# The last column block of a fused block's closing FFN: its products kept in row-block order, with the gate's row and two gated tiles prepared at other places

## The chip, the cores and the metric

The kernel runs on one core of one Trainium2 chip. The metric is the device time of one execution in microseconds (us). The median of three runs of the kernel before is 1876.98 us (1876.95 to 1877.79).

## The reference

A residual block works on x of 256 tokens by 2048 channels, in float32: a SwiGLU feed-forward, a mixer (mLSTM heads beside RG-LRU channels), and a second SwiGLU feed-forward. Each sublayer is modulated by shift, scale and gate computed from a conditioning vector c, and followed by a layer norm. What matters here is the second feed-forward and the norm that ends the block:

```python
g, v = jnp.split(u @ w13, 2, axis=-1)          # u = modulate(x, 2), w13: 2048 x 11264
y = (jax.nn.silu(g) * v) @ w2                  # w2: 5632 x 2048
x = _layer_norm(ALPHA * x + 0.5 * gate[:, 2] * y, ln_g[l, 2], ln_b[l, 2])
```

## The kernel before

Each float32 operand of a large product is split into a high part (a cast to fp32r on ScalarE, ACT) and a low part (the difference, on VectorE, DVE). A product of two operands is then three matmuls on TensorE (PE): high x high, high x low, low x high. A weight tile is 128 x 2048. It is loaded by a transfer that SyncE (SP) issues into a `raw` buffer (four of them) and split into a `hi` and a `lo` buffer (three of each).

`last_ffn` is the second feed-forward. Its 5632 hidden columns are 11 groups of 512. The tokens are two row blocks t = 0, 1 of 128 rows. `u2` holds the normalized, modulated and transposed input, as `uh` (high) and `ul` (low), 16 tiles of 128 channels. Groups 2 to 10 are computed by a Strassen-like scheme (`fast_group`). A string of steps gives PE's order within a group: `P1` to `P7` are sub-products of twelve matmuls each, `G` and `V` are plain sub-products of the gate's and value's columns (24 matmuls each), `X` takes a down tile of w2 (24 matmuls) from earlier groups, and `t` transposes a finished part of the hidden activations. `P1` reads u's tiles 0 to 3, `P2` and `P4` tiles 4 to 7, `G` 8 to 11, `V` 12 to 15; the other P's read sums of u that were made once before. Within a group, P1's raw tile sits in a `row` buffer (two of these; the modulation row and the gate's row take one each while they live) and is overwritten to make P5's, P6's and P4's operands, so it is free once P4's operand is split.

The order of the other engines' work in `last_ffn` comes from a planner, `Plan`, that runs when the kernel is built. Each operation is given with an engine (`T` PE, `V` DVE, `A` ACT, `G` POOL, `Q` SP), an assumed duration, what it reads and writes, and sometimes a due time (`by`). PE's operations keep the order in which they are written. For the others the planner works back due times from PE's, then schedules by list: among operations that could start, the one due first. It knows how many buffers of each kind there are. A load is assumed to land after 5.6 us (`LAND`). Each engine then gets its instructions in the order of the planned starts, and executes them in that order; nothing on the chip reorders between them. Instructions issued through `T`, `V`, `A`, `G` or `Q` are pinned to the written order. Those issued through `nc.tensor` are not: a scheduler orders them at build time by a simulated time line.

The output has four column blocks n of 512. Down tiles (n, k) of the last three groups (k = 0, 1, 2 for groups 8, 9, 10) are accumulated for n = 0, 1, 2 inside `last_ffn` (`end_tile`), multiplied by the gate, added to `yacc` (the residual, itself scaled by the gate and with alpha times x accumulated from DRAM), and their statistics are taken. For n = 3 the three weight tiles are multiplied by the gate's row (`gated`, and the lines after it for k = 0, as `l0`), split, and kept: k = 0 in `hi`/`lo` buffers, k = 1 and k = 2 in the place of `u2`, one half by row block each. The products of n = 3 are made in `boundary` (`last`, calling `mov_t`): `products(0)` for row block 0, then `products(1)`, 36 matmuls each. After a row block's products, DVE adds the sum to `yacc` (here also named x), takes statistics, and normalizes (`take`, `norm`), and the result goes out by eight transfers in all. For row block 1, two of its four columns are normalized through PE: `tz` receives x times ln_g through the identity, and then minus the mean times ln_g through a diagonal matrix `dm`, which ACT builds once the mean is known.

The gate's row (`gate_row`) is a PE transpose of the gate's columns, a scaling on ACT, and two transfers issued by POOL, through DRAM, that broadcast it to all partitions.

Of the kernel before, what the change touches and what calls it, by code (L numbers as in the profile page):

```python
# [44 lines left out]
DOUBLE = ()  # L45
ADA_END = 6
SLOT_END = 45.0
ADA_AT = tuple(2.0 + 8.0 * i for i in range(7)) + tuple(130.0 + 20 * i for i in range(9))

S4 = "P1 t X t P5 X P6 P3 X P7 P2 G P4 G X V V"  # L50
S2 = "P1 t G t P5 X P6 P3 G P7 P2 X P4 V V"
D6 = "P1 t X t P5 X P6 P3 X P7 P1 P2 X P5 P4 X P6 P3 P2 X P7 P4"


# [11 lines left out]

class Place:

    def __init__(self, tag, make, ap=None):
        self.tag, self.make, self.ap = tag, make, ap  # L70
        self.left, self.end, self.also, self.whole = 0, None, [], None

    def __call__(self):
        if self.ap is None:
            self.ap = self.make()
        return self.ap


# [9 lines left out]
class Plan:  # L88
# [11 lines left out]
        self.now = 0.0  # L100

    def place(self, tag, make, ap=None):
        p = Place(tag, make, ap)
        if ap is not None and tag:
            self.taken[tag] += 1
        return p

    def part(self, whole, key, make):
# [7 lines left out]
    def op(self, engine, dur, fn, reads=(), writes=(), moves=0.0, seq=None, by=None, at=None):  # L116
        s = Step(engine, dur, fn, moves)
        s.by = None if by is None else self.now + by
        s.at = at
        if engine == "T":  # L120
            s.due = self.now
            self.now += dur
            seq = "T"
        if seq:
            if seq in self.seq:
                s.order.add(self.seq[seq])
            self.seq[seq] = s
        keys = [[k for x in ks for k in (x, *(x.also if isinstance(x, Place) else ()))] for ks in (reads, writes)]
        for k in keys[0]:
            if k in self.last:  # L130
                s.before.add(self.last[k])
        for k in keys[1]:
            s.before.update(self.seen.get(k, ()))
            if k in self.last:
                s.before.add(self.last[k])
        for k in keys[0]:
            self.seen.setdefault(k, []).append(s)
        for k in keys[1]:
            self.last[k], self.seen[k] = s, []
        s.before.discard(s)  # L140
        for k in (*keys[0], *keys[1]):
            p = k[0] if isinstance(k, tuple) else k
            if isinstance(p, Place):
                p = p.whole or p
                if p.tag and p not in s.places:
                    s.places.add(p)
                    p.left += 1
                    if p.ap is None and not getattr(p, "used", False):
                        p.used = True
                        s.takes.append(p.tag)  # L150
        for b in s.before:
            b.after.add(s)
        self.steps.append(s)
        s.created = self.now
        return s

    def lasts(self, s):
        if s.moves:
            return self.LAND + (s.moves - 1.0) * self.EACH if s.moves > 1 else self.LAND
        return s.dur + self.GAP[s.engine]  # L160

    def run(self):
        for s in reversed(self.steps):
            if s.engine == "T":
                continue
            due = [t.due - self.lasts(s) for t in s.after]
            if s.by is not None:
                due.append(s.by - s.dur)
            if s.at is not None:
                due.append(s.at + self.AHEAD)  # L170
            s.due = min(due) if due else s.created + 8.0
            if s.at is not None:
                s.due = max(s.due, s.at + self.AHEAD)
        waiting = list(self.steps)
        mover = -20.0
        done = []
        while waiting:
            cands = {}
            seen_seq = set()
            for s in waiting:  # L180
                if any(b.end is None for b in s.before) or any(b.start is None for b in s.order):
                    continue
                t = max([self.free[s.engine], *(b.start + b.dur if b.engine == s.engine and not b.moves else b.end for b in s.before), *(b.start for b in s.order)])
                ok = True
                for tag in set(s.takes):
                    n = s.takes.count(tag)
                    spare = self.room[tag] - self.taken[tag] - len(self.gone[tag])
                    need = n - max(spare, 0)
                    if need > 0:
                        if len(self.gone[tag]) < need:  # L190
                            ok = False
                            break
                        t = max(t, sorted(self.gone[tag])[need - 1])
                if s.engine == "Q":
                    t = max(t, s.due - self.AHEAD)
                if ok:
                    cands.setdefault(s.engine, []).append((t, s))
            if not cands:
                for s in waiting[:12]:
                    print(s.engine, s.due, s.takes, [b.end is None for b in s.before])  # L200
                raise ValueError("no step can go")
            best = min(((t + s.dur, e) for e, c in cands.items() for t, s in c), key=lambda v: v[0])
            limit, e = best
            t, s = min(((t, s) for t, s in cands[e] if t < limit or t + s.dur <= limit), key=lambda v: (v[1].due, v[0]))
            s.start = t
            self.free[e] = t + s.dur
            if s.moves:
                mover = max(mover + s.moves * self.EACH, t + self.LAND + (s.moves - 1.0) * self.EACH)
                s.end = mover
            else:  # L210
                s.end = t + s.dur + self.GAP[e]
            for tag in s.takes:
                spare = self.room[tag] - self.taken[tag] - len(self.gone[tag])
                if spare <= 0:
                    self.gone[tag].remove(min(self.gone[tag]))
                self.taken[tag] += 1
            for p in s.places:
                p.left -= 1
                p.end = max(p.end or 0.0, s.end)
                if not p.left:  # L220
                    self.taken[p.tag] -= 1
                    self.gone[p.tag].append(p.end)
            waiting.remove(s)
            done.append(s)
        for s in sorted(done, key=lambda s: s.start):
            s.fn()
# [3 lines left out]
def block_kernel(ctx: ExitStack, tc: tile.TileContext, a: dict, out: bass.AP):  # L230
# [883 lines left out]
    def last_ffn(s, w13, w2):  # L1114
# [179 lines left out]
                           writes=[(y, n)], by=4.0)  # L1294
                yield

        def fast_group(b, quads, xs, steps):

            i = 8 * b
            single = quads == 1  # L1300
# [114 lines left out]
            for w in steps.split():  # L1415
                if w == "X":
                    next(xs)
                elif w == "t":
                    turn()
                else:  # L1420
                    q = count.get(w, 0)
                    count[w] = q + 1
                    hl = prep(w, q)
                    products(w, q, hl)
                    end(w, q)

        def ada(at):
            i, (s_, j, kt) = todo.pop(0)
# [26 lines left out]
        for b in range(2, n_b - 1, 2):  # L1455
            kgs = (b - 2, b - 1)
            xs = x_tiles(kgs, range(4))
            if b in DOUBLE:
                if len(ws) == 1:
                    ws.append(sums(1, in_slot))  # L1460
# [3 lines left out]
                for i in range(2):  # L1464
                    fast_group(b + i, 1, xs, S4)

        gate2 = gate_row()
        for t in range(NT):
            y = yacc[t]
            for n in range(4):  # L1470
# [20 lines left out]
                op("V", 0.65, lambda y=y, t=t: V.bn_stats(sts[t][:, n, :], y()[:, c]), reads=[(y, n)], writes=[("sts", t, n)],  # L1491
                   by=6.0)

        def gated(k):
            p = load(w2[kgs[k] * 4 + 3], f"w2{s}l{k}")
            for c in range(0, D, 512):
                op("V", 0.62, lambda c=c: V.tensor_mul(p()[:, c:c + 512], p()[:, c:c + 512], gate2()[:, 1536:]),
                   reads=[p, gate2], writes=[p])
            t = k - 1
            late = 30.0  # L1500
            into = [place(None, lambda w=w: half(t)()[w]) for w in range(2)]
            for h in into:
                h.also = [("u", k, t) for k in range(4)]
            hls[k] = [h() for h in split(p, "", into, late)]

        def first_tiles():
            for k in range(2):
                end_tile(0, k)
                yield

        fast_group(n_b - 1, 1, first_tiles(), S2)
        for i, (n, k) in enumerate(((1, 0), (1, 1), (2, 0), (0, 2), (1, 2), (2, 1), (2, 2))):
            end_tile(n, k)
            if i < 2:
                turn()
            if i in (0, 3):
                gated(1 + i // 3)
        p = load(w2[kgs[0] * 4 + 3], f"w2{s}l0")
        hl = [place(w, lambda w=w: wp.tile([P, 2048], F32R, tag=w, bufs=3, name=f"{w}l0")) for w in ("hi", "lo")]
        for c in range(0, D, 512):  # L1520
# [14 lines left out]

        def last(ps, t, n):
            for i in range(3):
                end = mov_t(ps, hls[i], *act_of(hts[kgs[i]]), 0, t, i == 0, i == 2)
            return end

        def act_of(h):
# [457 lines left out]
```

## Time and profile before

| what | value |
|---|---|
| median of three runs | 1876.98 us |
| profiled execution | 1877.39 us |
| its span, first to last instruction | 1875.6 us |
| mean granted PE clock | 0.998 |
| PE busy | 1858.3 us (99%) |
| PE weight loads busy | 1522.6 us |
| DVE busy | 1574.0 us (84%) |
| ACT busy | 902.5 us (48%) |
| moved by DMA | 520.06 MB, mean 277 GB/s |

The rows of the profile give a start and a duration in us, the engine, the line of the kernel, the operation, and output and inputs by their names. In `last_ffn` all operations are recorded at line 306, where the pinned engines issue; so one goes by tile names: `f` is a sum in a group, `tl` a sum of the last down tiles, `hfw`/`lfw` the high and low part of a group's weight tile (`lfw_100P` belongs to group 10 and a P step, `lfw_90P` to group 9), `hw`/`lw` those of a down tile, `rw22l` a raw tile of the last column block, `hil`/`lol` the parts of `l0`, and `u` in the last column block the gated tiles that lie in `u2`. Lines 465, 466 and 467 are the three matmuls of `mov_t`. A bracket gives the engine's idle time before the instruction, and what released it. Rows that begin with a stretch such as 1752.20:1804.90 give its length, then the busy time and the count of instructions of PE, PE's weight loads, DVE, ACT and POOL, then the granted PE clock, the DMA engines' share and GB/s. Matmuls overlap: a duration of 0.39 us does not mean that the next one starts 0.39 us later.

### The profile page before, as it was taken

How to read it: one execution, taken by the hardware profiler on the slowest of the kernel's cores; microseconds unless marked ns; L12 is line 12 of the kernel's file. 1: busy time of each engine (PE TensorE's matmuls, PEld its weight loads, DVE VectorE, ACT ScalarE, POOL GpSimd, SP SyncE). 2: the span in 40 equal slices, each digit the busy share in tenths (PEclk: the TensorE clock that was granted, in tenths of full speed). 3: DMA queues.
4: the chain of work that ended last, by engine and by line, in shares of the span. 5: the costliest groups of instructions: out<-in, count | busy, mean ns of one | idle time of the engine just before them, and what ended most of it. 6: DMA issues, size and time to landing. Idle time of an engine off the chain costs nothing.

```text
span 1875.6 us, 21251 instructions
## 1 busy us (share of the span) xinstructions
PE 1858.3 (99%) x8483; PEld 1522.6 (81%) x8483; DVE 1574.0 (84%) x1470; ACT 902.5 (48%) x854; POOL 43.8 (2%) x68
## 2 busy tenths in 40 slices
PE   8999999999999999999999999999999999999997
PEld 5788888888888888788888887888888888888885
DVE  6899998888887987889997787797889888777877
ACT  4543444533334335755744346645555455445541
POOL 0000000000000000100000021000000000000000
PEclk9999999999999999999999999999999999999999
DMA  9989889999999987377688573956646754555482
GB/s 377 415 355 367 313 310 356 356 344 355 349 361 357 340 336 269 138 277 287 247 318 302 195 260 143 363 221 245 258 186 274 289 204 158 202 224 214 176 266 85
DMA packets 74931, 520.06 MB, mean 277 GB/s; under 512 B 8736, under 2 KB 8912, under 8 KB 13520
## 3 DMA queue, kind: packets, MB, share of 16 engines
q1 hardware_dynamic: 72144, 507.54, 71.4%
q0 software_dynamic: 960, 7.37, 1.3%
q10 hardware_dynamic: 1728, 3.80, 0.6%
q8 instruction: 66, 1.08, 0.2%
q14 instruction: 33, 0.27, 0.0%
HBM read 514.46 MB, written 4.22 MB: 277 GB/s over the span
## 4 chain that ended last, share of the span: by engine, by line
PE 93%; DVE 3%; ACT 1%; DMA 1%; issue 1%; POOL 0%; SPq 0%; DVEq 0%; ACTq 0%
PE f L306 22%; PE py L306 9%; PE pj L454 5%; PE py L466 3%; PE py L465 3%; PE py L467 3%; PE pj L456 3%; PE tl L306 3%; PE fg L466 2%; PE fg L467 2%; PE fv L465 2%; PE fg L465 2%; PE fv L466 2%; PE fv L467 2%; PE rv L929 2%; PE rv L930 2%
## 5 line engine op out<-in xcount | busy, mean ns | idle before, releaser
L383 DVE CUSTOM_DVE_ANT_0 ada<-ada,scb,badac 128x2048 f32<-128x2048 f32 x94 | 220.5, 2345 | 16.7 <-DMA ada<-in_w_ada 16.3
L306 PE MATMUL py<-hw,ht 128*128 128x512 f32 x512 | 163.7, 391 | 0.0
L454 PE MATMUL pj<-u,hs 128*128 128x512 f32 x512 | 122.5, 391 | 0.0
L279 ACT CAST hra<-rra 128x2048 fp32r<-128x2048 f32 x38 | 72.6, 1915 | 101.8 <-DMA rra<-in_w_r 44.9
L279 ACT CAST hw<-rw 128x2048 fp32r<-128x2048 f32 x40 | 76.5, 1914 | 93.5 <-DMA rw<-in_w 50.9
L306 DVE TENSOR_TENSOR lw<-rw,hw 128x2048 fp32r<-128x2048 f32 x41 | 93.9, 2290 | 29.4 <-ACT hw L306 29.2
L306 ACT CAST hw<-rw 128x2048 fp32r<-128x2048 f32 x41 | 78.5, 1915 | 81.6 <-PE f L306 41.7
L306 PEld LDWEIGHTS py<-hw,ht 128*128 128x128 f32 x512 | 96.1, 188 | 19.8
L281 DVE TENSOR_TENSOR lw<-rw,hw 128x2048 fp32r<-128x2048 f32 x40 | 91.4, 2288 | 22.3 <-ACT hw L279 22.3
L454 PEld LDWEIGHTS pj<-u,hs 128*128 128x128 f32 x512 | 94.3, 188 | 18.4
L466 PE MATMUL py<-lw,hth 128*128 128x512 f32 x256 | 99.8, 390 | 0.1
L467 PE MATMUL py<-hw,htl 128*128 128x512 f32 x256 | 99.7, 389 | 0.0
L306 PE MATMUL py<-lw,ht 128*128 128x512 f32 x256 | 99.6, 389 | 0.0
L465 PE MATMUL py<-hw,hth 128*128 128x512 f32 x256 | 97.3, 392 | 0.0
L279 ACT CAST hs<-rs 128x2048 fp32r<-128x2048 f32 x32 | 61.0, 1908 | 69.3 <-PE pj L454 64.1
L306 DVE CUSTOM_DVE_ANT_0 ada<-ada,scb,badac 128x2048 f32<-128x2048 f32 (+1 forms) x40 | 87.3, 2184 | 3.1 <-DMA ada<-in_w_ada 2.7
L281 DVE TENSOR_TENSOR ls<-rs,hs 128x2048 fp32r<-128x2048 f32 x32 | 73.0, 2282 | 16.2 <-ACT hs L279 16.2
L306 DVE TENSOR_TENSOR lra<-rra,hra 128x2048 fp32r<-128x2048 f32 x29 | 66.3, 2285 | 8.9 <-ACT hra L306 6.8
L456 PEld LDWEIGHTS pj<-u,ls 128*128 128x128 f32 x512 | 65.6, 191 | 2.5
L456 PE MATMUL pj<-u,ls 128*128 128x256 f32 x512 | 66.4, 283 | 0.0
L279 ACT CAST hfg<-rfg 128x2048 fp32r<-128x2048 f32 x20 | 38.3, 1915 | 56.0 <-DMA rfg<-in_w 55.4
L281 DVE TENSOR_TENSOR lfv<-rfv,hfv 128x2048 fp32r<-128x2048 f32 x20 | 45.8, 2289 | 20.6 <-ACT hfv L279 20.6
(839 smaller groups left out, 4984.7 us busy)
## 6 DMA issues: line engine op xcount, KB each, us to landing
ada<-in_w_ada SPq DMA_DIRECT2D x128, 1024.0 KB, 6.8
rw<-in_w SPq DMA_DIRECT2D x81, 1024.0 KB, 6.7
rra<-in_w_r SPq DMA_DIRECT2D x45, 1024.0 KB, 7.5
rs<-in_w_s SPq DMA_DIRECT2D x32, 1024.0 KB, 5.1
rfv<-in_w SPq DMA_DIRECT2D x27, 1024.0 KB, 6.0
rfw<-in_w SPq DMA_DIRECT2D x27, 1024.0 KB, 5.1
rfg<-in_w SPq DMA_DIRECT2D x24, 1024.0 KB, 6.2
rwo<-in_w_out SPq DMA_DIRECT2D x16, 1024.0 KB, 4.8
```

The source lines that it names most:

```text
L279: act.copy(cut(hi, w), like(raw[:, w], hi))
L281: low.tensor_sub(cut(lo, w), like(raw[:, w], lo), cut(hi, w).bitcast(F32))
L306: self.last = getattr(self.engine, op)(*args, **kw)
L383: vec.tensor_tensor_reduce(raw[:, c], raw[:, c], scb[:, c], 1.0, base, ALU.mult, ALU.add, to)
L454: nc.tensor.matmul(ps, hi[:, k * P:(k + 1) * P], both(k), start=k == 0, stop=False)
L456: nc.tensor.matmul(ps[:, 0:S], lo[:, k * P:(k + 1) * P], uh[:, k, :], start=False, stop=k == KT - 1)
L465: pe.matmul(o, acth[:, k0 + j, tk], cut(hi, w), start=first and j == 0, stop=False, **kw)
L466: pe.matmul(o, acth[:, k0 + j, tk], cut(lo, w), start=False, stop=False, **kw)
L467: end = pe.matmul(o, actl[:, k0 + j, tk], cut(hi, w), start=False, stop=last and j == 3, **kw)
L929: pe.matmul(pss[t], uh[:, k0 + j, tk], hi[:, w], start=go, stop=False)
L930: pe.matmul(pss[t], uh[:, k0 + j, tk], lo[:, w], start=False, stop=False)
```

## The change

- The last column block's products are issued through `T`, so PE takes them as written: all 36 of row block 0 and then all 36 of row block 1.
- `gate_row()` is written before group 8 and not after group 9.
- The two gated tiles k = 1, 2 go into `u2` by its channel tiles and not by row block: k = 1 into tiles 0 to 7, k = 2 into tiles 8 to 15. So k = 1 may be written once P4 of group 10 is done, and k = 2 once group 10's V's are done. Their splits get due times 14 us after P4 and 20 us after the last V.
- Group 10 has an order of its own, `S10`: P2 and P4 come directly after P3, and P7 after the second X.
- A place in the planner may name several kinds of buffers, of which the one that is free first is taken (`choice`). All places of this kernel name one.

```diff
 S2 = "P1 t G t P5 X P6 P3 G P7 P2 X P4 V V"
+S10 = "P1 t G t P5 X P6 P3 P2 P4 G X P7 V V"
...
+    def choice(self, s):
+        t, used, out = -99.0, {}, []
+        for p in s.takes:
+            best = None
+            for tag in p.tags:
+                n = used.get(tag, 0)
+                spare = self.room[tag] - self.taken[tag] - len(self.gone[tag]) - n
+                if spare > 0:
+                    at = -99.0
+                elif len(self.gone[tag]) > -spare:
+                    at = sorted(self.gone[tag])[-spare]
+                else:
+                    continue
+                if best is None or at < best[0]:
+                    best = at, tag
...
-        def fast_group(b, quads, xs, steps):
+        def fast_group(b, quads, xs, steps, then={}):
...
                     end(w, q)
+                    then.get(w, lambda: None)()
...
             xs = x_tiles(kgs, range(4))
+            if b == n_b - 3:
+                gate2 = gate_row()
...
-        gate2 = gate_row()
...
-        def gated(k):
+        def gated(k, by):
             p = load(w2[kgs[k] * 4 + 3], f"w2{s}l{k}")
...
-            t = k - 1
-            late = 30.0
-            into = [place(None, lambda w=w: half(t)()[w]) for w in range(2)]
+            into = [place(None, lambda w=w: rows(8 * (k - 1))()[w]) for w in range(2)]
             for h in into:
-                h.also = [("u", k, t) for k in range(4)]
-            hls[k] = [h() for h in split(p, "", into, late)]
+                h.also = [("u", 2 * (k - 1) + i, t) for i in range(2) for t in range(NT)]
+            hls[k] = [h() for h in split(p, "", into, by - plan.now)]
...
-        fast_group(n_b - 1, 1, first_tiles(), S2)
+        fast_group(n_b - 1, 1, first_tiles(), S10, {"P4": lambda: gated(1, plan.now + 14.0)})
+        gated(2, plan.now + 20.0)
         for i, (n, k) in enumerate(((1, 0), (1, 1), (2, 0), (0, 2), (1, 2), (2, 1), (2, 2))):
             end_tile(n, k)
             if i < 2:
                 turn()
-            if i in (0, 3):
-                gated(1 + i // 3)
...
-                end = mov_t(ps, hls[i], *act_of(hts[kgs[i]]), 0, t, i == 0, i == 2)
+                end = mov_t(ps, hls[i], *act_of(hts[kgs[i]]), 0, t, i == 0, i == 2, T)
```

More of the change, by code (lines that the diff above doesn't have):

```diff
@@ L47 @@
 SLOT_END = 45.0
-ADA_AT = tuple(2.0 + 8.0 * i for i in range(7)) + tuple(130.0 + 20 * i for i in range(9))
+ADA_AT = tuple(2.0 + 8.0 * i for i in range(7)) + tuple(130.0 + 20.0 * i for i in range(9))
 S4 = "P1 t X t P5 X P6 P3 X P7 P2 G P4 G X V V"
 S2 = "P1 t G t P5 X P6 P3 G P7 P2 X P4 V V"
+S10 = "P1 t G t P5 X P6 P3 P2 P4 G X P7 V V"
 D6 = "P1 t X t P5 X P6 P3 X P7 P1 P2 X P5 P4 X P6 P3 P2 X P7 P4"
@@ L67, with __init__ @@
 class Place:
-    def __init__(self, tag, make, ap=None):
-        self.tag, self.make, self.ap = tag, make, ap
-        self.left, self.end, self.also, self.whole = 0, None, [], None
+    def __init__(self, tags, make, ap=None):
+        self.tags, self.make, self.ap = tags, make, ap
+        self.left, self.end, self.also, self.whole, self.tag, self.asked = 0, None, [], None, None, False
     def __call__(self):
         if self.ap is None:
-            self.ap = self.make()
+            self.ap = self.make(self.tag) if self.tag else self.make()
         return self.ap
@@ L102, in place @@
     def place(self, tag, make, ap=None):
-        p = Place(tag, make, ap)
-        if ap is not None and tag:
-            self.taken[tag] += 1
+        tags = (tag,) if isinstance(tag, str) else tag
+        p = Place(tags, (lambda _: make()) if isinstance(tag, str) else make, ap)
+        if ap is not None and tags:
+            p.tag, p.asked = tags[0], True
+            self.taken[p.tag] += 1
         return p
@@ L144, in op @@
                 p = p.whole or p
-                if p.tag and p not in s.places:
+                if p.tags and p not in s.places:
                     s.places.add(p)
                     p.left += 1
-                    if p.ap is None and not getattr(p, "used", False):
-                        p.used = True
-                        s.takes.append(p.tag)
+                    if not p.asked:
+                        p.asked = True
+                        s.takes.append(p)
         for b in s.before:
@@ L160, in lasts @@
         return s.dur + self.GAP[s.engine]
+    def choice(self, s):
[13 more added lines that the diff above has]
+                    best = at, tag
+            if best is None:
+                return None
+            t = max(t, best[0])
+            used[best[1]] = used.get(best[1], 0) + 1
+            out.append(best[1])
+        return t, out
     def run(self):
@@ L183, in run @@
                 t = max([self.free[s.engine], *(b.start + b.dur if b.engine == s.engine and not b.moves else b.end for b in s.before), *(b.start for b in s.order)])
[L184 to L193, printed above, removed]
+                got = self.choice(s)
+                if got is None:
+                    continue
+                t = max(t, got[0])
                 if s.engine == "Q":
                     t = max(t, s.due - self.AHEAD)
-                if ok:
-                    cands.setdefault(s.engine, []).append((t, s))
+                cands.setdefault(s.engine, []).append((t, s))
             if not cands:
                 for s in waiting[:12]:
-                    print(s.engine, s.due, s.takes, [b.end is None for b in s.before])
+                    print(s.engine, s.due, [p.tags for p in s.takes], [b.end is None for b in s.before])
                 raise ValueError("no step can go")
@@ L211, in run @@
                 s.end = t + s.dur + self.GAP[e]
[L212 to L216, printed above, removed]
+            if s.takes:
+                for p, tag in zip(s.takes, self.choice(s)[1]):
+                    p.tag = tag
+                    if self.room[tag] - self.taken[tag] - len(self.gone[tag]) <= 0:
+                        self.gone[tag].remove(min(self.gone[tag]))
+                    self.taken[tag] += 1
             for p in s.places:
```

## The prediction

> **What bounds the kernel now.** I read the page's busy row and its chain of work first, then TensorE's waits, then busy time by stage.
>
> ```profile
> PE 1858.3 (99%) x8483; PEld 1522.6 (81%) x8483; DVE 1574.0 (84%) x1470; ACT 902.5 (48%) x854; POOL 43.8 (2%) x68
> ...
> PE 93%; DVE 3%; ACT 1%; DMA 1%; issue 1%; POOL 0%; SPq 0%; DVEq 0%; ACTq 0%
> ```
> ```profile
> PE tz L306 <- ACT dm L306: 5.3, 1, 5.3
> ```
> ```profile
> 1752.20:1804.90 52.70, 52.70 (x238) 43.63 (x237) 45.08 (x32) 29.12 (x22) 2.87 (x4) 1.00 0.70 227
> 1804.90:1843.80 38.90, 38.90 (x178) 32.21 (x177) 33.14 (x39) 14.75 (x12) 0.00 (x0) 1.00 0.57 205
> 1843.80:1860.20 16.40, 16.40 (x74) 13.59 (x73) 10.05 (x14) 1.91 (x1) 0.57 (x1) 1.00 0.00 0
> 1860.20:1875.60 15.40, 5.57 (x9) 1.66 (x7) 10.55 (x17) 0.60 (x2) 2.80 (x4) 0.75 0.41 136
> ```
>
> TensorE (PE) carries 93% of the chain and is busy without a gap through group 10 (1752.2 to 1804.9), the nine other down tiles (to 1843.8) and the last column block (to 1860.2). The change removes no matmul, so nothing before 1860.2 can become shorter. What can is the last 15.4 us, where PE has ended its products and VectorE (DVE) still normalizes. PE's longest wait of the whole run is there. How that tail comes about is seen in the order of the products:
>
> ```profile
> 1843.79 0.62 PE L465 MATMUL tl<-hil,ht 128*128 128x512 f32 x2
> ...
> 1850.14 0.39 PE L466 MATMUL tl<-lol,ht 128*128 128x512 f32 x1
> ...
> 1857.39 0.39 PE L467 MATMUL tl<-u,ht 128*128 128x512 f32 x1
> ...
> 1859.88 0.40 PE L467 MATMUL tl<-u,ht 128*128 128x512 f32 x1
> 1860.12 1.88 PE L306 MATMUL tz<-yacc,ident 128*128 128x512 f32 x4
> ```
> ```profile
> 1850.24 2.29 DVE L306 TENSOR_TENSOR u<-rw22l,u 128x2048 fp32r<-128x2048 f32 x1 [1.98 <-ACT u L306]
> 1852.45 1.29 DVE L306 TENSOR_TENSOR yacc<-yacc,ln_g 128x512 f32<-128x512 f32 x2
> 1857.82 0.69 DVE L306 TENSOR_TENSOR yacc<-yacc,tl 128x512 f32<-128x512 f32 x1 [4.08 <-PE tl L467]
> ...
> 1862.22 2.73 DVE L306 SCALAR_TENSOR_TENSOR yacc<-yacc,rsp,ln_b 128x512 f32<-128x512 f32 x4
> 1864.87 0.68 DVE L306 TENSOR_TENSOR yacc<-yacc,tl 128x512 f32<-128x512 f32 x1
> ...
> 1869.80 0.74 DVE L306 SCALAR_TENSOR_TENSOR yacc<-tz,rsp,ln_b 128x512 f32<-128x512 f32 x1
> 1871.12 0.75 DVE L306 SCALAR_TENSOR_TENSOR yacc<-tz,rsp,ln_b 128x512 f32<-128x512 f32 x1 [0.57 <-PE tz L306]
> ```
>
> The 72 products mix both row blocks. PE's start times (L466 on `lol` again at 1850.14) show block 1's products between block 0's, because the third tile's low part was ready only at 1850.24 + 2.29 = 1852.5. Block 0's sum is complete at 1857.39 + 0.39 = 1857.78, and DVE takes it at 1857.82. Block 0 costs DVE 1864.87 - 1857.82 = 7.05 us, so block 1, complete at 1859.88 + 0.40 = 1860.28, waits till 1864.87. Those 4.6 us, with DVE on the chain, are what can be won.
>
> **The change part by part.**
>
> *Products row block by row block.* One product takes (1859.88 - 1843.79) / 71 = 0.2266 us. With PE held to the written order, block 0's 36th product starts at 1843.79 + 35 x 0.2266 = 1851.72 and ends 0.39 later, at 1852.11. DVE starts at 1852.15, ends block 0 at 1852.15 + 7.05 = 1859.20, and is free 1.1 us before block 1 is complete at 1860.28. DVE takes block 1 at 1860.32 and not at 1864.87: 4.55 us. DVE's own product of x and ln_g (1.29 us at 1852.45) must be over by 1852.15. It follows the third tile's split, which moves away; next ahead of it stands the last plain tile's eviction, six operations of 0.69 from 1843.8, so it is over near 1843.8 + 4.1 + 1.3 = 1849.2: 3 us of cover.
>
> *The second pair on `tz`.* After block 1's mean, ACT builds a diagonal and PE multiplies ln_g by it:
>
> ```profile
> 1866.85 0.40 ACT L306 ACTIVATE dm<-ident,nbn 128x128 f32<-128x128 f32 x1
> ```
> ```profile
> L306 PE MATMUL tz<-yacc,ident x4: 592/592/592, 1860.1 to 1861.4; 128*128 128x512 f32 x4
> ...
> L306 PE MATMUL tz<-ln_g,dm x4: 1057/1057/1219, 1867.3 to 1870.0; 128*128 128x512 f32 x4
> ```
> ```profile
> 1863.00:1864.00 1.00, 0.00 (x0) 0.00 (x0) 1.00 (x2) 0.00 (x0) 0.00 (x0) 1.00 0.15 55
> 1864.00:1865.00 1.00, 0.00 (x0) 0.00 (x0) 1.00 (x3) 0.00 (x0) 0.00 (x0) 0.82 1.07 375
> 1865.00:1866.00 1.00, 0.00 (x0) 0.00 (x0) 0.96 (x2) 0.00 (x0) 0.00 (x0) 0.50 1.04 315
> ```
>
> PE's last work before the wait ends at 1860.12 + 1.88 = 1862.00. The granted clock (third last column) is still 1.00 up to 1864 and 0.50 from 1865; a mean of 0.82 puts the fall at 1864.64, after 2.6 us of idleness. Hence 1057 ns instead of 592, and DVE's last operation waits 0.57 us for it. After the change the diagonal is done 2.38 us after DVE takes block 1 (1867.25 - 1864.87), at 1862.70: PE has been idle for 0.7 us. Between the ends "592" and "1057" I take 592, as 0.7 is well under 2.6. The pair then ends near 1862.70 + 1.88 = 1864.6, before DVE asks for it (1860.32 + 4.93 = 1865.25), and the 0.57 us go too. At half clock the gain stays 4.55. What follows DVE's last operation (1875.6 - 1871.87 = 3.7 us, the last transfer to the output) stays.
>
> [...]
>
> *The gate's row.* It moves ahead of group 8, some two groups earlier: one PE transpose, one ACT operation, two POOL transfers, and what hangs on it.
>
> ```profile
> 1752.16 0.11 PE adag L306
> ```
> ```profile
> L306 DVE TENSOR_TENSOR yacc<-yacc,gate x8: 682/684/686, 1779.8 to 1791.9; 128x512 f32<-128x512 f32 x8
> ```
> ```profile
> yacc<-xd POOLq DMA_DIRECT2D x2, 1024.0 KB, 10.1
> ...
> gate<-rowd POOLq DMA_DIRECT2D x1, 1024.0 KB, 4.9
> ```
>
> PE pays 0.11 us elsewhere: zero. POOL has nothing else queued. The eight products of yacc (8 x 0.684 = 5.5 us of DVE) and the two accumulating transfers (10.1 us each) may go earlier. They cost DVE the same wherever they stand, their next reader is the eviction of a tile that ends after 1820, and in any gap of DVE they are free. The row takes one of two "row" buffers for groups 8 to 10, so each group's first tile waits for the previous group's:
>
> ```profile
> 1721.49 0.43 SPq L306 DMA_DIRECT2D rfw<-in_w  x1
> 1726.56 0.33 SPq L306 DMA_DIRECT2D rfw_100G<-in_w  x1
> ```
> ```profile
> 1721.99 2.29 DVE L306 TENSOR_TENSOR lfw_90P<-rfw,hfw_90P 128x2048 fp32r<-128x2048 f32 x1 [0.91 <-ACT hfw_90P L306]
> ```
> ```profile
> 1741.37 1.91 ACT L306 CAST hfw_100P<-rfw 128x2048 fp32r<-128x2048 f32 x1 [2.32 <-issue]
> ```
>
> Group 10's load went out at 1721.49; now it goes after group 9's P4 split frees the buffer, at 1724.28, 2.8 us later. On SP the next load follows at 1726.56, so nothing queues behind it. Landing within 10 us (below) gives 1734, and the cast is at 1741.37: hidden, with 7 us to spare.
>
> *Two gated tiles into halves of u, in group 10's new order.* No operation is added: per tile one load, four products by the gate (0.68 us each), one cast (1.91), one subtraction (2.29). The first moves from the stage after 1804.9 into group 10 (it may be written into u after P4, whose end, counted at 2.72 us per twelve products from 1752.3, moves from 1794 to 1780.4); the second to before about 1825. Room on DVE:
>
> ```profile
> 1757.90:1777.70 19.80, 19.80 (x91) 16.41 (x90) 19.14 (x10) 11.53 (x10) 0.00 (x0) 1.00 0.57 205
> 1777.70:1804.90 27.20, 27.20 (x122) 22.53 (x121) 22.22 (x19) 13.14 (x9) 1.79 (x2) 1.00 0.86 254
> ```
>
> In 1777.7 to 1804.9 come 4 x 0.68 + 2.29 = 5.0 us and go up to 5.5 us of yacc: it fits. The tight place is before it: P6 P3 P2 P4 now run back to back, 2.72 us each, with three buffer pairs. P4's cast must wait for P6's products. The nearest case is P2's of before, released by P3:
>
> ```profile
> 1774.63 0.39 PE L306 MATMUL f<-hfw_100P,ws 128*128 128x512 f32 x1
> ```
> ```profile
> 1775.06 1.92 ACT L306 CAST hfw_100P<-rfw 128x2048 fp32r<-128x2048 f32 x1 [0.32 <-PE f L306]
> ```
> ```profile
> 1777.01 2.29 DVE L306 TENSOR_TENSOR lfw_100P<-rfw,hfw_100P 128x2048 fp32r<-128x2048 f32 x1
> ```
>
> From release (1775.02) to low part done (1779.30) is 4.28 us; P3 and P2 give 24 x 0.2266 = 5.44. Slack 1.1 us. A subtraction of 2.29 begun just before on DVE, or a 0.59 us copy first on ACT, would stall PE by up to 2.29 + 0.59 - 1.1 = 1.8. Bounds 0 and 1.8; I take 0, because the stage rows show PE busy all through 1752.2 to 1843.8 under the same planner, which orders by due time. A stall would be paid in full at the end. The change also adds a wait to ACT: the first gated tile's cast waits for P4's last product, and behind it stand the casts of P7 and V. ACT is busy 13.14 of 27.20 us there, so one cast of 1.91 held there is covered.
>
> *The planner's rewriting* (a place may name several kinds of buffers) changes no decision, as every place here names one.
>
> **The sum.** 4.55 + 0.57 = 5.1 us. The profiled execution took 1877.39 with a span of 1875.6; these become 1872.3 and 1870.5. Three runs have a median of 1876.98, 0.41 under it: 1871.9. A change within 0.2% (3.75 us) can hardly be told from none, so the limit for "faster" is 1873.2.
>
> **The rivals.**
>
> Four P's stall PE, by 0.3 to 1.8 us: 1872.2 to 1873.7. For it: DVE is 19.14 of 19.80 us busy there, and P4's subtraction comes into it. Against: P7's can leave it.
>
> Half clock for the second pair: 1872.4. For it: the only pair in this place took 1057 ns.
>
> The third tile is not made earlier after all (the change does not do what it says). A written order then makes PE wait for 1852.5 where it wants that tile at 1843.79 + 24 x 0.2266 = 1849.2: 3.3 us lost, 1875.2. Against: its place in u is free from 1804.9 on.
>
> Slower than before: the first gated tile's load lands late and its four products stand at the head of DVE's queue, with the splits of the V tiles behind them.
>
> ```profile
> DMA to landing us min/median/max: 4.7/5.5/8.7
> ...
> DMA to landing us min/median/max: 6.9/7.8/9.8
> ```
>
> These are the `rw` and `fw` tiles from 1600 us on. The planner counts 5.6 (LAND), so a landing of 9.8 is 4.2 late, less 1.1 slack: 3.1 us of stall, 1875.0. It becomes slower than before beyond 5.6 + 1.1 + 5.1 = 11.8 us, and by over 0.2% beyond 15.6 (1880.8), which only other contention, such as the moved accumulations of 10.1 us each, could bring.
>
> **Chances.** Forecast 64%; four P's 16% (11 of them under 1873.2); half clock 5%; something more gained, as yacc's products leave DVE freer, 2%; third tile or a late landing between 1873.2 and 1880.7: 8%; slower 5%. So faster 64 + 11 + 5 + 2 = 82%, same 5 + 8 = 13%, slower 5%. The range 1871.0 to 1873.8 holds the forecast with the runs' spread (0.8 us), half clock and the stalls to 1.8.
>
> **What would show it.** Right: PE starts its 37th product of the last block after DVE's addition of block 0's sum becomes possible, near 1852; DVE's two additions of `tl` lie about 8.2 us apart (7.05 before); the second pair takes 592 ns at clock 1.00; PE's waits list nothing new between 1625 and 1860; both gated subtractions end before 1830. Wrong: a PE wait on a `hfw_100P` or `lfw_100P`, on `u`, or a last product later than 1860.

## The result, and the profile after

The change takes 1872.22 us (median of ten runs, 1872.13 to 1872.47) against 1877.14 (ten runs): 4.9 us less, a ratio of 0.9973 with a 95% interval of 0.9964 to 0.9983. 1871.9 was forecast. The profiled execution has a span of 1870.5 us (1875.6 before).

First PE's longest waits after the change, then busy time by stage in the same columns as before (length; PE, weight loads, DVE, ACT, POOL; PE clock, DMA share, GB/s):

```profile
PE rg L326 <- ACT u L326: 2.1, 2, 1.7
PE pc L326 <- POOL ident masks.py:199: 1.4, 1, 1.4
PE tu L326 <- ACT n L326: 1.0, 1, 1.0
PE tz L326 <- ACT dm L326: 0.8, 1, 0.8
```
```profile
1752.20:1804.90 52.70, 52.70 (x238) 43.66 (x237) 44.89 (x32) 30.96 (x23) 0.87 (x1) 1.00 0.64 220
1804.90:1843.80 38.90, 38.90 (x178) 32.20 (x177) 31.71 (x37) 14.60 (x12) 0.00 (x0) 1.00 0.45 163
1843.80:1860.20 16.40, 16.40 (x73) 13.48 (x72) 11.39 (x19) 0.00 (x0) 1.69 (x2) 1.00 0.15 48
1860.20:1870.50 10.30, 3.53 (x8) 1.06 (x6) 5.66 (x9) 0.60 (x2) 1.69 (x2) 0.81 0.39 127
```

PE is as busy as before up to 1860.2: no stall has come into group 10. The last stage shrank from 15.4 to 10.3 us, and in the stage before it DVE works 11.39 us, not 10.05: block 0's normalization has moved under PE's products. PE's wait for `dm` fell from 5.3 to 0.8 us.

The time line of the end, PE first, then DVE:

```profile
1843.54 0.39 PE L326 MATMUL tl<-hil,ht 128*128 128x512 f32 x1
...
1851.70 0.39 PE L326 MATMUL tl<-hil,ht 128*128 128x512 f32 x1
...
1859.87 1.88 PE L326 MATMUL tz<-yacc,ident 128*128 128x512 f32 x4
1862.50 1.98 PE L326 MATMUL tz<-ln_g,dm 128*128 128x512 f32 x4 [0.76 <-ACT dm L326]
```
```profile
1851.90 0.69 DVE L326 TENSOR_TENSOR yacc<-yacc,tl 128x512 f32<-128x512 f32 x1 [3.88 <-PE tl L326]
...
1856.30 2.73 DVE L326 SCALAR_TENSOR_TENSOR yacc<-yacc,rsp,ln_b 128x512 f32<-128x512 f32 x4
1860.07 0.69 DVE L326 TENSOR_TENSOR yacc<-yacc,tl 128x512 f32<-128x512 f32 x1 [1.03 <-PE tl L326]
...
1863.67 1.41 DVE L326 SCALAR_TENSOR_TENSOR yacc<-yacc,rsp,ln_b 128x512 f32<-128x512 f32 x2 [0.44 <-POOL rsp L326]
1865.00 1.40 DVE L326 SCALAR_TENSOR_TENSOR yacc<-tz,rsp,ln_b 128x512 f32<-128x512 f32 x2
```
```profile
L326 PE MATMUL tz<-ln_g,dm x4: 592/592/697, 1862.5 to 1863.9; 128*128 128x512 f32 x4
```

Block 1's first product stands at 1851.70, right after block 0's last. DVE takes block 0 at 1851.90 and block 1 at 1860.07, where DVE now waits 1.03 us for PE, and the finished sum no longer waits for DVE. The second pair on `tz` takes 592 ns a matmul (1057 before), and DVE's last two operations follow each other without a wait.

The span's 5.1 us: block 1 is taken 4.80 us earlier (1864.87 to 1860.07). Of this 0.25 is not the change's, as PE starts the last block at 1843.54 in this execution and at 1843.79 in the one of before; a run below that keeps the old place of the gated tiles (the order alone) starts it at 1843.56 too. From there to DVE's end it takes 6.33 us (1866.40 - 1860.07) and not 7.00: 0.67. From DVE's end to the span's end it takes 4.10 us and not 3.73: 0.37 given back. 4.55 + 0.25 + 0.67 - 0.37 = 5.10. Without the 0.25 it is 4.85, close to the 4.92 between the medians.

### The profile page after: what moved, and what is told of

It is laid out like the page before. It is cut to its first block, busy times and chain, and to the rows that moved or that the text cites. A ratio compares the mean times of both kernels' runs of the same rounds, so it can differ in the third digit from the quotient of the medians.

```text
span 1870.5 us, 21255 instructions
## 1 busy us (share of the span) xinstructions
PE 1857.2 (99%) x8483; PEld 1522.9 (81%) x8483; DVE 1573.4 (84%) x1470; ACT 902.4 (48%) x854; POOL 43.7 (2%) x68
## 3 DMA queue, kind: packets, MB, share of 16 engines
q8 instruction: 66, 1.08, 0.2%
## 4 chain that ended last, share of the span: by engine, by line
PE 93%; DVE 3%; DMA 1%; ACT 1%; issue 1%; POOL 0%; POOLq 0%; DVEq 0%; SPq 0%; ACTq 0%
PE f L326 22%; PE py L326 9%; PE pj L474 5%; PE tl L326 3%; PE py L486 3%; PE py L487 3%; PE py L485 3%; PE pj L476 3%; PE fg L486 2%; PE fv L486 2%; PE fg L487 2%; PE fg L485 2%; PE fv L487 2%; PE fv L485 2%; PE rv L949 2%; PE rv L950 2%
## 5 line engine op out<-in xcount | busy, mean ns | idle before, releaser
L486 PE MATMUL fg<-lfg,u 128*128 128x512 f32 x160 | 62.5, 391 | 0.1
```

The source lines that it names most:

```text
L486: pe.matmul(o, acth[:, k0 + j, tk], cut(lo, w), start=False, stop=False, **kw)
```

## The experiments

Theory: the whole gain comes from row block 0 being complete early, which needs both the order of the products and a third tile that is ready when that order wants it; the half clock is a small second term. Rivals: the order alone brings it; or the new plan of groups 8 to 10 does. All ratios are to the kernel before, run on the same chip.

**The order alone** (kernel before, one edit):

```diff
-                end = mov_t(ps, hls[i], *act_of(hts[kgs[i]]), 0, t, i == 0, i == 2)
+                end = mov_t(ps, hls[i], *act_of(hts[kgs[i]]), 0, t, i == 0, i == 2, T)
```

> The kernel before, with one edit: the last column block's products are issued through the pinned PE, so all 36 of row block 0 come first; the gated tiles stay where they were. My theory (the gain is order times readiness): before, the third tile's low part ended at 1852.5, and PE in the written order wants it at 1849.2, so PE stalls 3.3 us and all that follows shifts by that; the gain is 4.8 - 3.3 = 1.5 us plus at most 0.6 of the half clock: about 1875.3 (1875.0 to 1875.6), with a new PE wait of about 3.3 us on u. Rival A (the order alone brings the gain): 1872.2. Rival B (the gain comes from the new plan of groups 8 to 10, not from the order): 1877.1 or above.

Measured: 1877.29 us (1876.41 to 1878.35), ratio 1.0003 (0.9994 to 1.0012). No gain at all, less than my theory left. PE's time line in its profiled run, the clock (third last column), and DVE's taking of block 1:

```profile
1846.28 2.88 PE L306 MATMUL tl<-u,ht 128*128 128x512 f32 x12
1850.03 0.51 PE L306 MATMUL tl<-u,ht 128*128 128x512 f32 x1 [0.87 <-ACT u L306]
1852.36 5.06 PE L306 MATMUL tl<-u,ht 128*128 128x512 f32 x11 [1.82 <-DVE u L306]
1857.22 0.63 PE L306 MATMUL tl<-hil,ht 128*128 128x512 f32 x1
```
```profile
1851.00:1852.00 1.00, 0.00 (x0) 0.00 (x0) 1.00 (x1) 0.00 (x0) 0.00 (x0) 0.73 0.00 0
...
1853.00:1855.00 2.00, 2.00 (x6) 1.60 (x5) 0.51 (x1) 0.00 (x0) 0.00 (x0) 0.50 0.00 0
1855.00:1857.00 2.00, 2.00 (x6) 1.53 (x5) 0.00 (x0) 0.00 (x0) 0.00 (x0) 0.50 0.00 0
1857.00:1858.00 1.00, 1.00 (x3) 0.78 (x3) 0.54 (x1) 0.00 (x0) 0.00 (x0) 0.50 0.00 0
1858.00:1859.00 1.00, 1.00 (x5) 0.81 (x4) 0.93 (x3) 0.00 (x0) 0.00 (x0) 0.85 0.00 0
```
```profile
1866.09 0.69 DVE L306 TENSOR_TENSOR yacc<-yacc,tl 128x512 f32<-128x512 f32 x1 [1.50 <-PE tl L306]
```

The stall for the third tile came as worked out, to 1852.36; PE sat idle for the last 1.82 us of it, though block 1's products on the two ready tiles came later in its order. What I had left out is PE's clock: it fell near 1851.5 and came back only near 1858.3, and 11 products that should take 2.5 us at 0.2266 us each took from 1852.36 to 1857.22. DVE took block 1 at 1866.09, 6.0 us later than in the changed kernel. This profiled run is the longest of the eleven; by the medians the order-only kernel is 5.1 us longer than the changed one.

**The order alone, with PE kept at work in the stall**, to test that reading:

```diff
+                if t == 0 and i == 1:
+                    idle(bank(f"warm{s}"), 10)
```

> The run with the written order alone, plus 10 matmuls of the identity on a spare bank after the second tile's products of block 0, which fill PE's stall before the third tile; no result uses them. My theory of the order-only run: of the 6 us by which it fell short of the change, 3.1 are PE's stall for the third tile (1849.0 to 1850.0 and 1850.3 to 1852.4) and 3 are the half clock that the stall brings, from 1851.5 to 1858.3. With PE kept at work the clock stays at 1.00, block 1 is taken near 1863.1 and not 1866.1, and the time is about 3 us shorter: 1874.0 to 1874.6. If the half clock there has another cause: 1877.3 stays.

Measured: 1875.61 us (1875.41 to 1875.92), ratio 0.9992 (0.9983 to 1.0001).

```profile
1849.14 2.39 PE L306 MATMUL warm<-ident 128*128 128x128 f32 x20
1851.29 0.48 PE L306 MATMUL tl<-u,ht 128*128 128x512 f32 x1
1852.49 2.80 PE L306 MATMUL tl<-u,ht 128*128 128x512 f32 x11 [0.72 <-DVE u L306]
```
```profile
1853.00:1855.00 2.00, 2.00 (x10) 1.61 (x10) 0.64 (x2) 0.00 (x0) 0.00 (x0) 1.00 0.00 0
```
```profile
1863.50 0.69 DVE L306 TENSOR_TENSOR yacc<-yacc,tl 128x512 f32<-128x512 f32 x1 [1.03 <-PE tl L306]
```

The clock stays at 1.00, and the 11 products take 2.6 us (1852.49 to 1855.13). The span is 2.6 us shorter than that of the order-only profile (1874.0 against 1876.6), the median only 1.7: the order-only runs scatter over 1.9 us, in two groups (six from 1876.41 to 1877.29, five from 1878.11 to 1878.35), and its profiled run, at 1878.35, was its longest. That the work done at half clock differs from run to run would explain the scatter; only one of those runs has a trace, so this stays open. My 1874.0 to 1874.6 was too low: it took 3 us off the median where the profile carried them.

**The tiles without the order** (changed kernel, products unpinned as before):

```diff
-                end = mov_t(ps, hls[i], *act_of(hts[kgs[i]]), 0, t, i == 0, i == 2, T)
+                end = mov_t(ps, hls[i], *act_of(hts[kgs[i]]), 0, t, i == 0, i == 2)
```

> The changed kernel with the last products no longer pinned, so that the build's scheduler orders them; the two gated tiles, the gate's row and group 10 stay as changed. My theory: that scheduler mixed the row blocks before only because the third tile was late in its time line; with all three tiles ready it takes block 0 first by itself: 1872.2 (to 1872.6), DVE's two additions of tl about 8.2 us apart. Rival A (pinning is what makes the order): the blocks mix again, block 0 complete near 1857, 1876 to 1877.

Measured: 1871.99 us, ratio 0.9972 (0.9962 to 0.9982): the whole gain without the pinned order. DVE takes block 0 at 1851.88 and block 1 at 1860.05; the build's scheduler puts block 0 first by itself when all three tiles are early.

**A mixed order with early tiles** (changed kernel; tile by tile, twelve products of block 0 and twelve of block 1):

```diff
...
+            for i in range(3):
+                for t in range(NT):
+                    end = mm(ps[t, 3], t, i)
...
```

> The changed kernel with the last products pinned in a mixed order: for each of the three tiles twelve products of block 0, then twelve of block 1. Same products, same early tiles. My theory: block 0 is complete only after 60 products, at 1843.54 + 59 x 0.2266 + 0.39 = 1857.3; DVE needs 7.05 us for it and takes block 1 at 1864.4, the second pair on tz runs at half clock again after about 5 us of idleness; 4.3 us plus 0.3 to 0.6 lost: 1876.5 to 1876.9. Rival B (the new plan of groups 8 to 10 brings the gain): stays at 1872.2.

Measured: 1876.81 us, ratio 0.9998 (0.9989 to 1.0007); the gain is gone though groups 8 to 10 are those of the changed kernel. DVE:

```profile
1857.29 0.69 DVE L326 TENSOR_TENSOR yacc<-yacc,tl 128x512 f32<-128x512 f32 x1 [9.32 <-PE tl L326]
...
1864.35 0.68 DVE L326 TENSOR_TENSOR yacc<-yacc,tl 128x512 f32<-128x512 f32 x1
```

Block 0 at 1857.29 (1857.3 expected), block 1 at 1864.35 (1864.4). The second pair on `tz` took 1058 ns a matmul, the half-clock time again (1057 before). The order of the products carries the gain, and the plan of groups 8 to 10 brings none of its own.

**The second pair by itself** (kernel before, PE kept at work through most of its last wait):

```diff
+                idle(bank(f"warm{s}"), 16)
```

> The kernel before with 16 more matmuls of the identity on a spare bank after the first pair on tz, which keep PE at work for some 3.8 us of its 5.3 us wait; no result uses them. My theory: the second pair on tz then runs at 592 ns and not 1057, DVE's last operation loses its 0.57 us wait, but the last output transfers, which then come closer together, give some of it back: 1876.6 to 1876.9, against 1877.1. If the half clock is not from idleness: 1057 ns stays and 1877.1. If the transfers take nothing back: 1876.5.

Measured: 1876.74 us, ratio 1.0000 (0.9991 to 1.0009); the difference cannot be told from none by time. The trace shows both halves of the expectation, though:

```profile
1869.50 1.41 DVE L306 SCALAR_TENSOR_TENSOR yacc<-tz,rsp,ln_b 128x512 f32<-128x512 f32 x2
```
```profile
L306 PE MATMUL tz<-ln_g,dm x4: 593/593/697, 1867.0 to 1868.4; 128*128 128x512 f32 x4
```

593 ns and no wait of DVE; its end, at 1870.91, is 4.09 us before the span's end (1875.0), as in the changed kernel, and not 3.73.

**Only the due time of the gated tiles** (kernel before: both are asked for right after group 10, and due 14 and 20 us after it; old halves, old row, old steps, unpinned):

```diff
         fast_group(n_b - 1, 1, first_tiles(), S2)
+        gated(1)
+        gated(2)
...
-            if i in (0, 3):
-                gated(1 + i // 3)
...
-            late = 30.0
+            late = 14.0 + 6.0 * t
```

> The kernel before, with one edit: the two gated tiles k = 1, 2 are asked for directly after group 10, due 14 and 20 us later, and not after the first and the fourth of the seven down tiles, due 30 us later. The halves of u by row block, the gate's row after group 9, group 10's old order and the unpinned products stay. My theory now (readiness of the third tile is the whole gain; in the run with the tiles of the change alone the build's scheduler took block 0 first by itself): about 1872.2 (1871.8 to 1872.8), block 0 complete near 1852. Rival A (the halves by channel tiles and group 10's new order are needed, since both tiles then fall into the busy stretch after 1804.9): PE waits on lw or u between 1805 and 1850, 1873 to 1876. Rival B (only pinning or the early row helps): 1877.

Measured: 1872.26 us, ratio 0.9975 (0.9965 to 0.9985). Asking for the tiles earlier, with an earlier due time, brings the gain of the whole change; the run does not tell these two apart. The third tile's low part, and block 0's and block 1's sums, in its trace:

```profile
1818.84 2.29 DVE L306 TENSOR_TENSOR u<-rw22l,u 128x2048 fp32r<-128x2048 f32 x1 [1.04 <-ACT u L306]
...
1852.26 0.69 DVE L306 TENSOR_TENSOR yacc<-yacc,tl 128x512 f32<-128x512 f32 x1 [4.33 <-PE tl L467]
...
1859.97 0.69 DVE L306 TENSOR_TENSOR yacc<-yacc,tl 128x512 f32<-128x512 f32 x1 [0.58 <-PE tl L467]
```

The tile is ready at 1821.1 instead of 1852.5. The two tiles fall into the stretch after 1800, and PE has no wait there.

**Group 10's old steps, and the row made late** (changed kernel, one part undone each):

```diff
-        fast_group(n_b - 1, 1, first_tiles(), S10, {"P4": lambda: gated(1, plan.now + 14.0)})
+        fast_group(n_b - 1, 1, first_tiles(), S2, {"P4": lambda: gated(1, plan.now + 14.0)})
```

> The changed kernel with group 10 in its old order of steps; all else as changed, so the first gated tile may be written only after P4 near 1794 and is due 14 us later. My theory: the first tile is wanted at 1846.3 and has 38 us to spare, so nothing changes: 1872.2 (1871.8 to 1872.6). Rival A (the new order is needed for room on DVE and ACT): a PE wait in 1790 to 1845, more than 0.5 us slower. Rival C (the new order itself costs something, the four P's in a row): faster than 1871.8.

```diff
-            if b == n_b - 3:
-                gate2 = gate_row()
...
+        gate2 = gate_row()
         for t in range(NT):
```

> The changed kernel with the gate's row made after group 9, as before. My theory: the row is there by about 1762, the first gated tile needs it near 1780, so the early row is not needed: 1872.2 (1871.8 to 1872.6). Rival A (its eight products of yacc, 5.5 us of DVE, then crowd the stretch after 1780): a PE wait there, 0.5 to 2 us slower.

Measured: 1872.21 us (ratio 0.9977, 0.9968 to 0.9986) and 1872.39 (0.9975, 0.9967 to 0.9984). Neither part is needed for this gain, and neither costs anything that these runs could tell.

**A shorter way to block 1's root** (changed kernel; the main lines, and besides them each column is normalized to its end before the next):

```diff
+                V.tensor_scalar(v, mv[:, 1:2], 1.0, EPS, op0=ALU.mult, op1=ALU.add)
+                V.reciprocal(v, v)
...
+                A.activation(r, v, AF.Sqrt)
```

> The changed kernel with row block 1's reciprocal root taken by DVE (add, reciprocal) and ACT (square root) in place of POOL's two operations (1.8 us from the mean to rsp), and with each column normalized to the end before the next. My theory of the end as it now is: 1 MB of block 1's output leaves at about 340 GB/s, 3 us from its first column on, so the first column's time counts; it comes 0.8 us earlier, DVE's last operation 0.2 to 0.4 us earlier, and the span shortens by 0.3 to 0.7: 1871.5 to 1871.9. If the end hangs on DVE's last operation alone: 1871.9 to 1872.1. If the square root on ACT costs a table load in this place: 1872.5 to 1873.5.

Measured: 1872.06 us, ratio 0.9974 (0.9964 to 0.9984), within the noise of the change itself. The root is there early, but DVE pays for it:

```profile
1859.81 0.69 DVE L326 TENSOR_TENSOR yacc<-yacc,tl 128x512 f32<-128x512 f32 x1 [1.03 <-PE tl L326]
...
1862.67 0.75 DVE L326 SCALAR_TENSOR_TENSOR yacc<-yacc,rsp,ln_b 128x512 f32<-128x512 f32 x1
...
1864.78 1.40 DVE L326 SCALAR_TENSOR_TENSOR yacc<-tz,rsp,ln_b 128x512 f32<-128x512 f32 x2
```

The first column's last operation starts at 1862.67, 2.86 us after block 1 is taken (3.60 in the changed kernel), but DVE ends 6.37 us after it (6.33): two more operations (0.15 and 0.17 us) and two dependent pairs, whose second operation starts 0.84 and 0.79 us after the first where independent ones here follow at 0.66, eat the 0.44 us of waiting. The span ends 4.0 us after that (4.1). So my theory of the end fell: a first column 0.7 us earlier was worth no more than 0.1 us here, and the time fits the other expectation, that the end hangs on DVE's last operation.

## Why the prediction was right

*Products in row-block order: right.* Block 0 was expected at DVE at 1852.15, block 1 at 1860.32; they came at 1851.90 and 1860.07, both 0.25 early with the start of the block. The two additions lie 8.17 us apart (8.2). 4.55 us was the size, and the mixed order takes it away again. Both gated tiles were ready long before, at 1792.2 and 1820.0:

```profile
1789.89 2.29 DVE L326 TENSOR_TENSOR u<-rw22l,u 128x2048 fp32r<-128x2048 f32 x1
...
1817.74 2.28 DVE L326 TENSOR_TENSOR u<-rw22l,u 128x2048 fp32r<-128x2048 f32 x1
```

*The second pair: right in mechanism, mis-sized.* After 0.76 us of idleness it ran at full clock, 592 ns a matmul (clock 1.00 from 1862 to 1865). The falls of the clock that the traces here show came 2.1 us or more after PE's last steady work (last section). DVE's part became 0.67 us shorter (0.57 expected). But the step "what follows DVE's last operation stays" failed: 3.73 became 4.10 us, most likely since the last two columns now leave 0.7 us apart and not 1.3. So the term of 0.57 us was worth a net 0.3. The kernel before with PE kept at work agrees: from block 1's taking to the span's end it needs 10.43 us, as the changed kernel does, against 10.73. The profiled spans came out at the forecast 5.1 us less only because 0.25 us of difference between two executions made up for this; that was luck. The transfers at the end of the changed kernel's trace:

```profile
1866.00:1867.00 1.00, 0.00 (x0) 0.00 (x0) 0.41 (x1) 0.00 (x0) 0.00 (x0) 0.78 1.07 338
1867.00:1868.00 1.00, 0.00 (x0) 0.00 (x0) 0.00 (x0) 0.00 (x0) 0.00 (x0) 0.50 1.08 332
```

They run at 332 to 338 GB/s with all DMA engines taken (shares of 1.07 and 1.08), and a column of 256 KB needs 0.78 us at that rate, more than the 0.7 between two columns.

*Group 10: right, with the slack as worked out.* P4's cast and low part:

```profile
1772.13 1.92 ACT L326 CAST hfw_100P<-rfw 128x2048 fp32r<-128x2048 f32 x1 [0.85 <-PE f L326]
```
```profile
1774.08 2.29 DVE L326 TENSOR_TENSOR lfw_100P<-rfw,hfw_100P 128x2048 fp32r<-128x2048 f32 x1 [0.48 <-ACT hfw_100P L326]
```

4.24 us from cast to low part (4.28 expected from release on). PE first reads the low part at 1777.55, 1.2 us after it is done, and has no wait. P7's sum and subtraction had left the place (1747.88 and 1784.17, against 1762.36 and 1774.77 before), as the rival's counter-argument said.

*The row buffer: right.* Group 10's first load went out when the buffer came free:

```profile
1724.22 0.33 SPq L326 DMA_DIRECT2D rfw<-in_w  x1
```

1724.28 was worked out, and nothing waited for it.

*The rivals.* A late third tile was priced at 3.3 us. Its mechanism exists, as the order-only run shows. Counted from the last block's start, block 1 is taken 3.3 us later than in the changed kernel when the clock is held ((1863.50 - 1843.69) - (1860.07 - 1843.54) = 3.28), so the wait itself was priced rightly. What the price lacked is the half clock that the stall brings: with it 6.0 us in the profiled run, 5.1 by the medians. Under a written order a late tile would have eaten the whole gain. It did not happen in the changed kernel because the tile was asked for in time.

What I did not see: that the due time alone would do. I took the pinned order as the cause and the tiles as its condition; the build's scheduler had mixed the blocks only because the tiles were late. The run with the due time alone moved both tiles at once. That the third one is what counted was not run by itself; it is argued from the rows of before, where block 1's products come in, at 1850.14, about where block 0 wanted the third tile (1849.2).

## What to carry to other kernels

Before an order is enforced, ask why it isn't taken: here the mixed order was a symptom of operands asked for late, and asking for them earlier brought the whole gain without the rest. An engine that does the same work in another order gains nothing itself; read instead which consumer gets its first complete result earlier, and whether the last one then waits for the producer and no longer for the consumer. A stall of PE must be priced with the clock it can cost: 3.3 us of waiting cost 6.0 in the profiled run and 5.1 by the medians.

## What the hardware showed that I had not expected

In these traces PE's clock did not fall after one fixed time without work. Where a 1 us row holds a change between 1.00 and 0.50, its mean gives the time of the change. Two more rows of the kernel before, beside the fall at 1864.64:

```profile
1871.00:1872.00 1.00, 0.08 (x1) 0.00 (x0) 0.75 (x1) 0.00 (x0) 0.00 (x0) 0.77 1.09 318
...
1874.00:1875.00 1.00, 0.00 (x0) 0.00 (x0) 0.00 (x0) 0.00 (x0) 0.00 (x0) 0.94 0.00 0
```

They give a return at 1871.46 and a second fall at 1874.88, 3.8 us after the end of PE's last work (1871.08). In the order-only run the clock falls at 1851.46 and returns at 1858.30. The half clock so lasted 6.82 us in the one trace and 6.84 in the other. The run with the due time alone, whose PE ends its last work at 1864.39, falls latest after it:

```profile
1864.00:1865.00 1.00, 0.39 (x1) 0.00 (x0) 1.00 (x3) 0.00 (x0) 0.00 (x0) 1.00 0.00 0
...
1868.00:1869.00 1.00, 0.00 (x0) 0.00 (x0) 0.00 (x0) 0.00 (x0) 0.00 (x0) 0.95 0.23 80
```

So in these traces the length of a wait does not tell by itself when the clock falls; what else decides was not shown. The clock fell 2.1 us after PE's last work in the changed kernel (1864.48 to 1866.56), 2.6 us after the last work before the wait in the kernel before, and 4.5 us after it in the run with the due time alone (1864.39 to 1868.90). In the order-only run one product even ran inside the stall (at 1850.03, 0.51 us), and the clock still fell 2.3 us after the last steady one (1849.16 to 1851.46). There 5.9 us of the half clock held products without a gap (from 1852.36). So that stall of some 3 us cost nearly as much again: 6.0 us in the profiled run, against 3.28 with the clock held.
